# Token-major products in groups of 512 columns, and the relative-position vector copied from DRAM to DRAM

## The chip, the cores and the metric

The kernel runs on one core of a Trainium2 chip as one program. Its metric is the device time of one execution in microseconds (us): 1580.26 us, the median of three runs from 1579.17 to 1581.57.

Six kinds of instruction stream appear in the profile. PE is TensorE with its matmuls, PEld its weight loads (a matmul's stationary operand, 128 rows by 128 columns), DVE is VectorE, ACT is ScalarE, POOL is GpSimd, and SP is the queue that issues most transfers. Each stream runs its own instructions in order and waits for others by semaphores. 16 DMA engines carry the transfers of all streams.

## The reference

Two networks of two layers each run one after the other on 256 tokens of width 1024. The first has a gated recurrence beside a sliding-window attention, a cross attention to 256 memory tokens, and a gated feed-forward part. The second is what follows, cut to its core:

```python
def diff_attention(q, k, v, lam, rel_bias):
    ...
    bucket = t5_bucket(k_pos[None, :] - q_pos[:, None])
    bias = rel_bias[bucket].transpose(2, 0, 1)          # 4 heads, a value per distance
    p = softmax(einsum(q_blk, kt) + bias)
    w = p[:, :, 0] - lam * p[:, :, 1]
    return w @ v

for l in range(2):                                       # second_block
    h = rms_norm(x, pre_norm[l])
    proj = h @ w_in[l]
    y_a = rms_norm(diff_attention(q, k, v, lam, rel_bias)) * silu(z_a)
    y_h = hyena(u_h, x1, x2, filters) * silu(z_h)        # two FFT convolutions
    m = sigmoid(g_a) * (y_a @ w_pa[l]) + sigmoid(g_h) * (y_h @ w_ph[l])
    x = x + rms_norm(m @ w_out[l], post_norm[l])
```

Nearly all of the arithmetic is products of the 256 tokens with float32 weight matrices that are read from DRAM once, some 230 MB in all. The bias of an attention depends only on the distance between key and query, so it is a vector of 512 values for each of 4 heads.

## The kernel before

**Products in three parts.** A float32 product is made of three fp32r matmuls. Each operand is split into a rounded high part and the low rest. `mm3` adds high by high, high by low and low by high into the same PSUM tile.

**The weight stream.** `run_stream` takes the program as one list of chunks of weights, 1 MB each. SP loads a chunk into one of three raw buffers (L211). A chunk has two halves. For each half, ACT writes the high part (`wh`, L229) and DVE the low part (`wl`, L231), 128 partitions by 1024 values, into one of four pairs of split buffers. Then PE consumes the half. So a transfer that is late reaches PE by way of ACT.

**Two forms of product.** `fm` makes channel-major results: the weights are the stationary operand and the 256 tokens move, so every matmul has 256 columns. `tm` makes token-major results (256 tokens in two tiles of 128, `tb`): the activations are stationary and the weights move. It goes over the weight matrix in groups of 256 columns. A chunk is one group with all eight blocks of 128 rows (`k`), and its two halves are four blocks each. In a group each `tb` gets one PSUM tile of 256 columns, filled by 24 matmuls, and then the function `evac` empties it.

**Where `tm` stands.** In each layer of the first network: the queries with keys and values (`evq`, 1280 columns), the cross attention's values (`cross_v`), the mixer's output and the cross attention's output (both `out_proj`, with the layer norm in `ln_evac`). In each layer of the second: values and gate (`evv`, 1024 columns) and the output product (`evo`). In the last group of a `tm`, tile `tb` 0 is finished first, so that its `evac` can run while PE works on tile 1 (`hold`).

**Order.** PE and SP run in the order in which the program is written out. Attention, convolutions and norms are coroutines that `pump` lets go on between the halves of chunks, by a clock `self.t` that adds up the matmuls' columns. The other engines' order is set by a scheduler from priorities. PSUM has two pools of four banks: `pst` for `fm`, and `pch` for `tm` tiles and coroutines.

**The bias.** `load_bias` runs as part of `prep_co` beside the feed-forward part of the first network's second layer. A one-hot matmul gives the tile `vec` in PSUM, 4 heads by 512 values, which DVE copies to SBUF. One transfer from POOL's queue (L1200) then writes each head's row 128 times to a DRAM scratch tensor, `scr`, with the heads outermost: 4 x 128 x 512 values, 1 MB. Two further transfers (L1206) read it back with a row step of 511 instead of 512, so that partition p gets the row shifted by p. They fill the `bias` slots that `diff_co` adds to the scores in both layers of the second network.

Of the kernel before, what the change touches and what calls it, by code (L numbers as in the profile page):

```python
# [13 lines left out]
F32 = mybir.dt.float32  # L14
# [89 lines left out]
class Net:  # L104
# [300 lines left out]

    def tm(self, w, c0, ncols, x, evac):

        for c in range(c0, c0 + ncols, 256):
            box = {}
            last = c + 256 == c0 + ncols  # L410
            ci = (c - c0) // 256

            def part(h, tb, wt, ps):
                xx = x()
                t = slice(tb * P, tb * P + P)
                if self.start:

                    for j in range(3):
                        for k in range(4):
                            self.mm(ps, self.ch2(xx, k, t)[j == 1], wt[j == 2][:, k, :],  # L420
                                    k == 0 and j == 0, False)
                    self.start = tb == 0
                    return
                for k in range(4):
                    g = h * 4 + k
                    self.mm3(ps, self.ch2(xx, g, t), (wt[0][:, k, :], wt[1][:, k, :]),
                             g == 0, g == KD - 1)

            def first(wh, wl, box=box, last=last, part=part):
                box["ps"] = [self.pch([256], "tm") for _ in range(TB)]  # L430
                box["w"] = wh, wl
                part(0, 0, (wh, wl), box["ps"][0])
                if not last:
                    self.pump()
                    part(0, 1, (wh, wl), box["ps"][1])

            def second(wh, wl, box=box, last=last, part=part, ci=ci):
                part(1, 0, (wh, wl), box["ps"][0])
                evac(ci, 0, box["ps"][0])
                self.pump()  # L440
                if last:
                    part(0, 1, box["w"], box["ps"][1])
                part(1, 1, (wh, wl), box["ps"][1])
                evac(ci, 1, box["ps"][1])
            yield Chunk([(None, w[:, c:c + 256].rearrange("(k p) f -> p k f", p=P))], KD, 256,
                        False, [first, second], hold=last)

    def rstd(self, out, ss, scale, eps):
        if scale == 1.0:
# [83 lines left out]
        nc.vector.tensor_scalar(nsp, ab, -8.0, None, op0=ALU.mult)  # L533
        return sp, nsp

    def ln_evac(self, t, h, n=256, f=1.0, gb=None, pause=False):


        nc = self.nc
        st = {}  # L540

        def ev(c, tb, ps):
            if c == 0 and tb == 0:
                for b in range(TB):
# [282 lines left out]
    def mixer(self, l, s):  # L827
# [5 lines left out]
        def evq(c, tb, ps):  # L833
            if c == 0 and tb == 0:
                s.q = [self.slot("q", [D]) for _ in range(TB)]
                kvt = self.slot("kv", [2, TB, 256])
                s.kv, s.kT = kvt[:, 0], kvt[:, 1]
            dst = s.kv[:, tb, :] if c == 4 else s.q[tb][:, c * 256:c * 256 + 256]
            nc.scalar.activation(dst, ps, AF.Copy)
        yield from self.tm(w, 2048, 1280, x, evq)  # L840

# [54 lines left out]
    def cross_v(self, l, s):  # L896
        def ev(c, tb, ps):
            if c == 0 and tb == 0:
                s.V = [self.hl("cv", [D]) for _ in range(TB)]
            sl = slice(c * 256, c * 256 + 256)  # L900
            self.split(s.V[tb][0][:, sl], s.V[tb][1][:, sl], ps)
        return self.tm(self.a["ckv_w"][l], 1024, 1024, lambda: self.memT, ev)

# [59 lines left out]
    def ffn(self, l, s):  # L963
# [19 lines left out]
        def up(j):  # L983
            for i, c in enumerate((j * 256, D_FF + j * 256)):
                def ev(_, ps, i=i):
                    pss[j, i] = ps
                    if i == 1:
                        act(j)
                yield from self.fm(wi, c, 256, lambda: s.fx, ev)

        ev_ln = self.ln_evac(lambda: s.t, lambda: s.h, 512,
                             gb=lambda: s.gb, pause=l == DEPTH - 1)

        def down(j):
# [193 lines left out]
    def load_bias(self):  # L1188
# [7 lines left out]
        self.mm(ps, rb, oh, True, True)  # L1196
        vec = self.tmp([512], "vec")[:4, :]
        nc.vector.tensor_copy(vec, ps)
        flat = self.dr.tile([4, (P + 1) * 512], F32, name="scr")
        nc.gpsimd.dma_start(flat[:, :P * 512].rearrange("h (p r) -> h p r", r=512),  # L1200
                            vec[:, None, :].to_broadcast([4, P, 512]))
        self.bias = []
        for hp in range(2):
            b = self.slot("bias", [2, 384])
# [385 lines left out]
    def layer2(self, l, s, out):  # L1590
# [22 lines left out]
        def evv(c, tb, ps):  # L1613
            if c == 0 and tb == 0:
                s.v, s.za = self.slot("v", [TB, 512]), self.slot("za", [TB, 512])
            sl = slice((c % 2) * 256, (c % 2) * 256 + 256)
            if c < 2:
                nc.scalar.activation(s.v[:, tb, sl], ps, AF.Copy)
            else:
                z = s.za[:, tb, sl]  # L1620
                nc.scalar.activation(z, ps, AF.Tanh, scale=0.5)
                nc.vector.scalar_tensor_tensor(z, z, 1.0, ps, op0=ALU.add, op1=ALU.mult)
        yield from self.tm(w, 1024, 1024, x, evv)
# [27 lines left out]
        def begin():  # L1651
            if l < DEPTH - 1:
                self.load_pre_gain(l + 1)
            s.pn = self.slot("pn", [D])
            nc.gpsimd.dma_start(s.pn, a["post_norm_2"][l:l + 1, :].to_broadcast([P, D]))
            s.ss = [self.sm.tile([P, 4], F32, tag="pss", name=self.nm("pss")) for _ in range(TB)]
            s.xo = [self.slot("xo", [D]) for _ in range(TB)]
        yield begin

        def evo(c, tb, ps):  # L1660
            sl = slice(c * 256, c * 256 + 256)
            xo = s.xo[tb]
            jk = self.tmp([256], "jk2")
            nc.scalar.activation(jk, ps, AF.Square, accum_out=s.ss[tb][:, c:c + 1])
            nc.vector.tensor_tensor(xo[:, sl], ps, s.pn[:, sl], op=ALU.mult)
            if c == 3:
                sm = self.tiny(1, "sm")
                nc.vector.reduce_sum(sm, s.ss[tb], axis=AX)
                self.rstd(sm, sm, 1.0 / D, 4e-6)
# [99 lines left out]
```

## Time and profile before

| what | value |
|---|---|
| median of three runs | 1580.26 us (1579.17 to 1581.57) |
| the profiled execution's own time | 1578.38 us |
| its span, first to last instruction | 1576.6 us |
| PE, PEld busy | 96%, 92% of the span |
| DVE, ACT, POOL busy | 70%, 55%, 5% |
| mean granted clock of TensorE, share of full speed | 0.988 |
| matmuls and transposes | 11740 |

The shares say which engine is occupied over the whole span; where it is not, and why, is read from the waits and from windows of time. The page also cuts the span into 40 slices of 39.4 us and gives a tenth of busy time for each. A matmul's duration in the rows covers its pipeline from end to end, so that two that follow one another overlap; what one costs is read from the distance between the starts.

### The profile page before, as it was taken

To read this page: it belongs to the slowest core of one execution; us is meant where nothing else is said; L and a number is where in the kernel's file an instruction comes from. 1 tells how busy PE (TensorE), PEld (TensorE's weight loads), DVE (VectorE), ACT (ScalarE), POOL (GpSimd) and SP (SyncE) were. 2 spreads that over 40 slices of the span, in tenths; PEclk is the share of its full clock that TensorE was granted. 3 is DMA by queue.
4 is the path that set the end of the run, shared out by engine and by line. 5 is a ranking of instruction groups with operands and counts; after the bars stand their busy time and mean duration, and the time that the engine had idled before them with its cause. 6 is when DMAs were issued, how large, how long until landed. Compare 5 with 4: busy or idle time off the path is not lost. (4 is left out here: it accounts for less than half of the span.)

```text
span 1576.6 us, 28159 instructions
## 1 busy us (share of the span) xinstructions
PE 1513.9 (96%) x11740; PEld 1446.1 (92%) x11740; DVE 1103.9 (70%) x1642; ACT 867.7 (55%) x1378; POOL 83.5 (5%) x151
## 2 busy tenths in 40 slices
PE   8999999999999999999999999948999999999997
PEld 7889999999999999899999989947799899898997
DVE  5867677667655578767777875514897978797865
ACT  5789444535444446794446466513545665555753
POOL 4001000000000000010000200000000010000000
PEclk9999999999999999999999999978999999999999
DMA  9434755545555554356564775536355346354452
GB/s 278 135 122 147 234 179 177 165 157 201 175 186 188 187 161 155 108 180 214 187 187 161 208 217 184 183 69 206 110 165 171 120 154 208 128 166 140 142 167 80
DMA packets 228304, 264.09 MB, mean 168 GB/s; under 512 B 6231, under 2 KB 213305, under 8 KB 228176
## 3 DMA queue, kind: packets, MB, share of 16 engines
q1 hardware_dynamic: 221808, 246.43, 48.6%
q0 software_dynamic: 6368, 15.85, 4.2%
q8 instruction: 92, 1.51, 0.4%
q14 instruction: 36, 0.29, 0.1%
HBM read 260.16 MB, written 2.10 MB: 166 GB/s over the span
## 5 line engine op out<-in xcount | busy, mean ns | idle before, releaser
L231 DVE TENSOR_TENSOR wl<-raw,wh 128x1024 fp32r<-128x1024 f32 x464 | 568.1, 1227 | 326.0 <-ACT wh L229 321.2
L229 ACT ACTIVATE wh<-raw 128x1024 fp32r<-128x1024 f32 (+1 forms) x465 | 490.4, 1058 | 468.5 <-PE fm L361 241.9
L361 PE MATMUL fm<-h2h,wh 128*128 128x256 f32 x704 | 172.6, 286 | 27.5 <-ACT wh L229 27.5
L361 PE MATMUL fm<-n2h,wh 128*128 128x256 f32 x640 | 176.6, 286 | 1.2 <-ACT n2h L350 1.2
L361 PE MATMUL fm<-n2l,wh 128*128 128x256 f32 x640 | 174.8, 283 | 1.4 <-DVE n2l L351 1.4
L361 PE MATMUL fm<-n2h,wl 128*128 128x256 f32 x640 | 174.5, 283 | 0.0
L361 PE MATMUL fm<-h2h,wl 128*128 128x256 f32 x704 | 171.7, 285 | 0.5 <-DVE wl L231 0.5
L361 PE MATMUL fm<-h2l,wh 128*128 128x256 f32 x704 | 171.6, 285 | 0.4 <-DVE h2l L351 0.4
L361 PEld LDWEIGHTS fm<-h2h,wh 128*128 128x128 f32 x704 | 124.5, 194 | 32.0 <-ACT wh L229 27.9
L361 PEld LDWEIGHTS fm<-h2h,wl 128*128 128x128 f32 x704 | 123.5, 194 | 0.8 <-DVE wl L231 0.8
L361 PEld LDWEIGHTS fm<-h2l,wh 128*128 128x128 f32 x704 | 123.5, 194 | 0.6 <-DVE h2l L351 0.6
L361 PEld LDWEIGHTS fm<-n2h,wh 128*128 128x128 f32 x640 | 119.9, 192 | 3.3 <-ACT n2h L350 1.7
L361 PEld LDWEIGHTS fm<-n2l,wh 128*128 128x128 f32 x640 | 119.8, 192 | 1.8 <-DVE n2l L351 1.8
L361 PEld LDWEIGHTS fm<-n2h,wl 128*128 128x128 f32 x640 | 119.9, 192 | 0.2
L361 PE MATMUL tm<-wh,mgl 128*128 128x256 f32 x256 | 72.5, 283 | 0.7 <-DVE mgl L351 0.7
L361 PE MATMUL tm<-wl,mgh 128*128 128x256 f32 x256 | 72.4, 283 | 0.0
L361 PE MATMUL tm<-wh,mgh 128*128 128x256 f32 x256 | 72.4, 283 | 0.0
L361 PE MATMUL fm<-xTh,wh 128*128 128x256 f32 x256 | 70.9, 287 | 0.0
L361 PE MATMUL fm<-h3h,wh 128*128 128x256 f32 x256 | 70.8, 287 | 0.0
L361 PE MATMUL fm<-h3h,wl 128*128 128x256 f32 x256 | 69.8, 283 | 0.0
L361 PE MATMUL fm<-xTh,wl 128*128 128x256 f32 x256 | 69.8, 283 | 0.0
L361 PE MATMUL fm<-h3l,wh 128*128 128x256 f32 x256 | 69.8, 283 | 0.0
(432 smaller groups left out, 4073.3 us busy)
## 6 DMA issues: line engine op xcount, KB each, us to landing
raw<-in_w_in_dram SPq DMA_DIRECT2D x89, 1024.0 KB, 5.3
raw<-in_ffn_wi_dram SPq DMA_DIRECT2D x44, 1024.0 KB, 5.2
raw<-in_ffn_wo_dram SPq DMA_DIRECT2D x22, 1024.0 KB, 5.0
raw<-in_w_out_dram SPq DMA_DIRECT2D x16, 1024.0 KB, 5.3
raw<-in_ckv_w_dram SPq DMA_DIRECT2D x16, 1024.0 KB, 5.3
raw<-in_w_br_attn_dram SPq DMA_DIRECT2D x8, 1024.0 KB, 5.4
raw<-in_w_br_rnn_dram SPq DMA_DIRECT2D x8, 1024.0 KB, 5.3
raw<-in_cq_w_dram SPq DMA_DIRECT2D x8, 1024.0 KB, 5.2
```

The source lines that it names most:

```text
L229: hi_ins = self.nc.scalar.activation(hi[:, i:i + q], s[:, i:i + q], AF.Copy)
L231: lo_ins = self.nc.vector.tensor_tensor(lo, s, hi.bitcast(F32), op=ALU.subtract)
L361: self.nc.tensor.matmul(out, lhsT=l, rhs=r, start=start, stop=stop)
```

## The change

Two places change. In `load_bias`, `vec` is first written to a small DRAM tensor, `row`, of 4 x 512 values (8 KB). The transfer into `scr` then reads `row` instead of the SBUF tile and has the 128 copies outermost, the heads second.

In `tm` a group has 512 columns where 512 are left (the 1280 columns of `evq` become 512, 512 and 256). A chunk of a 512-column group has four blocks of 128 rows, so that it is 1 MB as before, and a group takes two chunks. Each half has two blocks. The functions that empty PSUM handle 512 columns at a time, and the norms' partial sums get half as many parts.

```diff
-        for c in range(c0, c0 + ncols, 256):
+        end = c0 + ncols
+        for gi, c in enumerate(range(c0, end, 512)):
+            wd = min(512, end - c)
+            nk = 2048 // wd
             box = {}
-            last = c + 256 == c0 + ncols
-            ci = (c - c0) // 256
...
-                for k in range(4):
-                    g = h * 4 + k
-                    self.mm3(ps, self.ch2(xx, g, t), (wt[0][:, k, :], wt[1][:, k, :]),
-                             g == 0, g == KD - 1)
+                for i in range(n):
+                    k = g * n + i
+                    self.mm3(ps, self.ch2(xx, k, t), (wt[0][:, i, :], wt[1][:, i, :]),
+                             k == 0, k == KD - 1)
...
+            def half(g, hold, wh, wl, box=box, part=part, gi=gi, wd=wd, nk=nk):
+                n_half = 2 * KD // nk
+                if g == 0:
+                    box["ps"] = [self.pch([wd], "tm") for _ in range(TB)]
+                part(g, 0, (wh, wl))
+                if hold and g == n_half - 2:
+                    box["w"] = wh, wl
+                    return
+                if g == n_half - 1:
+                    evac(gi, 0, box["ps"][0])
                 self.pump()
-                if last:
-                    part(0, 1, box["w"], box["ps"][1])
-                part(1, 1, (wh, wl), box["ps"][1])
-                evac(ci, 1, box["ps"][1])
+                if hold and g == n_half - 1:
+                    part(g - 1, 1, box["w"])
+                part(g, 1, (wh, wl))
+                if g == n_half - 1:
+                    evac(gi, 1, box["ps"][1])
+            for ck in range(KD // nk):
+                hold = c + wd == end and ck == KD // nk - 1
+                src = w[ck * nk * P:(ck + 1) * nk * P, c:c + wd]
...
-    def ln_evac(self, t, h, n=256, f=1.0, gb=None, pause=False):
+    def ln_evac(self, t, h, n=512, f=1.0, gb=None, pause=False):
...
+        one = self.dr.tile([4, 512], F32, name="row")
+        nc.gpsimd.dma_start(one, vec)
         flat = self.dr.tile([4, (P + 1) * 512], F32, name="scr")
-        nc.gpsimd.dma_start(flat[:, :P * 512].rearrange("h (p r) -> h p r", r=512),
-                            vec[:, None, :].to_broadcast([4, P, 512]))
+        nc.gpsimd.dma_start(flat[:, :P * 512].rearrange("h (p r) -> p h r", r=512),
+                            one[None, :, :].to_broadcast([P, 4, 512]))
...
-            sl = slice(c * 256, c * 256 + 256)
+            sl = slice(c * 512, c * 512 + 512)
             xo = s.xo[tb]
-            jk = self.tmp([256], "jk2")
+            jk = self.tmp([512], "jk2")
```

What this does to the order of the engines is shown at three places. The first is POOL's stream around the bias, before the change (`scr` and `bias` as above, `up` the borders of the second network's convolution inputs):

```order
L1191 DMA oh_11401<-in_c_bucket_dram 32x512
L1200 DMA scr<-vec_11491 4x128x512
L1501 MEMSET up_12258 128x2
...
L1502 MEMSET up_12611 128x2
L1206 DMA bias_11495<-scr 128x2x384
L1206 DMA bias_11497<-scr 128x2x384
```

And the same place after it:

```order
L1200 DMA oh_10545<-in_c_bucket_dram 32x512
L1210 DMA row<-vec_10635 4x512
L1212 DMA scr<-row 128x4x512
L1218 DMA bias_10641<-scr 128x2x384
L1218 DMA bias_10643<-scr 128x2x384
L1513 MEMSET up_11404 128x2
```

There is one transfer more, the large one has 128 as its first size instead of 4, and the two that read the copies back stand right behind it, ahead of the borders.

The second place is PE's stream at the start of the first layer's output product (`tm` the PSUM tile of a token tile, `wh` and `wl` the weights' parts, `mgh` and `mgl` the activations'), before the change:

```order
L361 MATMUL tm_2678<-wh_2571,mgh_2469 128x256
L361 MATMUL tm_2678<-wl_2572,mgh_2469 128x256
L361 MATMUL tm_2678<-wh_2571,mgl_2471 128x256
...
L361 MATMUL tm_2679<-wh_2571,mgh_2469 128x256
L361 MATMUL tm_2679<-wl_2572,mgh_2469 128x256
...
L361 MATMUL tm_2678<-wh_2603,mgh_2470 128x256
```

And after it:

```order
L361 MATMUL tm_2574<-wh_2467,mgh_2365 128x512
L361 MATMUL tm_2574<-wl_2468,mgh_2365 128x512
L361 MATMUL tm_2574<-wh_2467,mgl_2367 128x512
...
L361 MATMUL tm_2575<-wh_2467,mgh_2365 128x512
L361 MATMUL tm_2575<-wl_2468,mgh_2365 128x512
...
L361 MATMUL tm_2574<-wh_2499,mgh_2365 128x512
```

A tile now gets six matmuls of 512 columns from a half where it got twelve of 256. Over the program 2400 `tm` matmuls of 256 columns become 1152 of 512 and 96 of 256; nothing else on PE changes its order.

The third place is DVE's stream at the end of the same product (`t` the sum with the residual, `bst` the statistics, `mv` and `rs` mean and scale), before the change:

```order
L548 SCALAR_TENSOR_TENSOR t_2676<-x_99,tm_2808 128x256
L550 BN_STATS bst_2720<-t_2676 128x6
L548 SCALAR_TENSOR_TENSOR t_2677<-x_100,tm_2809 128x256
L550 BN_STATS bst_2721<-t_2677 128x6
L231 TENSOR_TENSOR wl_2867<-raw_2670,wh_2866 128x1024
L548 SCALAR_TENSOR_TENSOR t_2676<-x_99,tm_2872 128x256
L550 BN_STATS bst_2720<-t_2676 128x6
L553 BN_AGGR mv_2900<-bst_2720 128x2
```

And after it:

```order
L231 TENSOR_TENSOR wl_2645<-raw_2503,wh_2644 128x1024
L231 TENSOR_TENSOR wl_2665<-raw_2566,wh_2664 128x1024
L231 TENSOR_TENSOR wl_2681<-raw_2566,wh_2680 128x1024
L557 SCALAR_TENSOR_TENSOR t_2572<-x_99,tm_2650 128x512
L559 BN_STATS bst_2632<-t_2572 128x6
L562 BN_AGGR mv_2700<-bst_2632 128x2
```

The last sum and statistics before the mean now cover 512 columns each, and the sums of the third quarter no longer stand ahead of them.

## Rows read from the trace of the kernel before

**Rows 1.** The page: engine busy time, share and instruction count.
```profile
PE 1513.9 (96%) x11740; PEld 1446.1 (92%) x11740; DVE 1103.9 (70%) x1642; ACT 867.7 (55%) x1378; POOL 83.5 (5%) x151
```

**Rows 2.** The page's 40 slices: granted clock and DMA share, in tenths.
```profile
PEclk9999999999999999999999999978999999999999
DMA  9434755545555554356564775536355346354452
```

**Rows 3.** PE's waits: line, releaser, us in total, times, longest.
```profile
PE fm L361 <- ACT wh L229: 27.5, 1, 27.5
...
PE dft L361 <- DVE dsc L1420: 3.5, 2, 1.8
PE tx L373 <- DVE xn L1579: 2.3, 1, 2.3
PE tx L373 <- DVE t L562: 2.1, 3, 1.4
```

**Rows 4.** Timeline of ACT: start us, us, instruction, idle before and releaser.
```profile
1070.43 2.01 ACT L229 ACTIVATE wh<-raw 128x1024 fp32r<-128x1024 f32 x2 [36.04 <-DMA raw<-in_ffn_wi_dram]
```

**Rows 5.** DMA issues: queue, count, KB each, median us to landing.
```profile
raw<-in_ffn_wi_dram SPq DMA_DIRECT2D x44, 1024.0 KB, 5.2
...
fdl<-in_flt_deltas_dram POOLq DMA_DIRECT2D x4, 512.0 KB, 8.2
...
scr<-vec POOLq DMA_DIRECT2D x1, 1024.0 KB, 47.5
...
bias<-scr POOLq DMA_DIRECT2D x2, 384.0 KB, 5.8
...
fb<-in_flt_bias_dram POOLq DMA_DIRECT2D x4, 2.0 KB, 2.8
```

**Rows 6.** Timeline of SP and POOL: issues around the wait.
```profile
1022.41 1.13 POOL L1200 DMA_DIRECT2D scr<-vec  x1 [83.76 <-DVE vec L1198]
...
1023.27 6.60 SPq L211 DMA_DIRECT2D raw<-in_ffn_wi_dram  x2
```

**Rows 7.** Windows: from:to us, busy us (instructions) PE, PEld, DVE, ACT, POOL, clock, DMA, GB/s.
```profile
1044.00:1065.00 21.00, 0.04 (x1) 0.00 (x0) 0.00 (x0) 0.00 (x0) 0.00 (x0) 0.59 0.27 32
...
1071.00:1078.00 7.00, 6.00 (x26) 5.70 (x27) 5.83 (x6) 3.96 (x5) 0.13 (x2) 0.50 0.47 165
```

**Rows 8.** Timeline of PE after the wait, first row and first at full pace.
```profile
1071.54 0.80 PE L361 MATMUL fm<-h2h,wh 128*128 128x256 f32 x2 [27.50 <-ACT wh L229]
...
1078.51 0.29 PE L361 MATMUL fm<-h2h,wl 128*128 128x256 f32 x1
```

**Rows 9.** Chain that ended last: start us, us, engine, tile, instructions.
```profile
1193.25 10.08 PE tm L361 x84
...
1544.51 20.18 PE tm L361 x168
```

**Rows 10.** Timeline of PE in the feed-forward part's 512-column matmuls.
```profile
1104.81 0.39 PE L361 MATMUL ff<-wh,al 128*128 128x512 f32 x1
...
1110.02 0.39 PE L361 MATMUL ff<-wl,ah 128*128 128x512 f32 x1
```

**Rows 11.** Groups by shape: count, busy us, mean ns, idle before.
```profile
L550 DVE BATCH_NORM_STATS2 bst<-t 128x6 f32<-128x256 f32 x32 | 13.6, 426 | 1.0
...
L548 DVE SCALAR_TENSOR_TENSOR t<-t,tm 128x256 f32<-128x256 f32 x24 | 9.8, 410 | 1.7 <-PE tm L361 1.7
...
L548 DVE SCALAR_TENSOR_TENSOR t<-t,ff 128x512 f32<-128x512 f32 x8 | 5.2, 673 | 0.0
...
L550 DVE BATCH_NORM_STATS2 bst<-t 128x6 f32<-128x512 f32 x8 | 5.1, 679 | 0.0
```

**Rows 12.** The same view of ACT.
```profile
L350 ACT ACTIVATE cqh<-fm 128x512 fp32r<-128x512 f32 x8 | 4.8, 598 | 14.5 <-PE fm L361 14.5
...
L1664 ACT ACTIVATE jk<-tm 128x256 f32<-128x256 f32 x16 | 6.2, 385 | 17.0 <-PE tm L361 17.0
```

More of the change, by code (lines that the diff above doesn't have):

```diff
@@ L406, in tm, with part @@
     def tm(self, w, c0, ncols, x, evac):
-        for c in range(c0, c0 + ncols, 256):
+        end = c0 + ncols
+        for gi, c in enumerate(range(c0, end, 512)):
+            wd = min(512, end - c)
+            nk = 2048 // wd
             box = {}
-            last = c + 256 == c0 + ncols
-            ci = (c - c0) // 256
-            def part(h, tb, wt, ps):
+            def part(g, tb, wt, box=box, nk=nk):
                 xx = x()
+                ps = box["ps"][tb]
                 t = slice(tb * P, tb * P + P)
+                n = nk // 2
                 if self.start:
                     for j in range(3):
-                        for k in range(4):
+                        for k in range(n):
                             self.mm(ps, self.ch2(xx, k, t)[j == 1], wt[j == 2][:, k, :],
@@ L423, in part @@
                     return
-                for k in range(4):
-                    g = h * 4 + k
-                    self.mm3(ps, self.ch2(xx, g, t), (wt[0][:, k, :], wt[1][:, k, :]),
-                             g == 0, g == KD - 1)
[L429 to L435, printed above, removed]
@@ L437, in second @@
-            def second(wh, wl, box=box, last=last, part=part, ci=ci):
-                part(1, 0, (wh, wl), box["ps"][0])
-                evac(ci, 0, box["ps"][0])
-                self.pump()
-                if last:
-                    part(0, 1, box["w"], box["ps"][1])
-                part(1, 1, (wh, wl), box["ps"][1])
-                evac(ci, 1, box["ps"][1])
-            yield Chunk([(None, w[:, c:c + 256].rearrange("(k p) f -> p k f", p=P))], KD, 256,
-                        False, [first, second], hold=last)
+                for i in range(n):
+                    k = g * n + i
+                    self.mm3(ps, self.ch2(xx, k, t), (wt[0][:, i, :], wt[1][:, i, :]),
+                             k == 0, k == KD - 1)
@@ L448, in rstd @@
+            for ck in range(KD // nk):
+                hold = c + wd == end and ck == KD // nk - 1
+                src = w[ck * nk * P:(ck + 1) * nk * P, c:c + wd]
+                yield Chunk([(None, src.rearrange("(k p) f -> p k f", p=P))], nk, wd, False,
+                            [lambda wh, wl, f=half, g=2 * ck + h, o=hold: f(g, o, wh, wl)
+                             for h in range(2)], hold=hold)
     def rstd(self, out, ss, scale, eps):
@@ L837, in evq @@
                 s.kv, s.kT = kvt[:, 0], kvt[:, 1]
-            dst = s.kv[:, tb, :] if c == 4 else s.q[tb][:, c * 256:c * 256 + 256]
+            dst = s.kv[:, tb, :] if c == 2 else s.q[tb][:, c * 512:c * 512 + 512]
             nc.scalar.activation(dst, ps, AF.Copy)
@@ L989, in up @@
                 yield from self.fm(wi, c, 256, lambda: s.fx, ev)
-        ev_ln = self.ln_evac(lambda: s.t, lambda: s.h, 512,
+        ev_ln = self.ln_evac(lambda: s.t, lambda: s.h,
                              gb=lambda: s.gb, pause=l == DEPTH - 1)
@@ L1615, in evv @@
                 s.v, s.za = self.slot("v", [TB, 512]), self.slot("za", [TB, 512])
-            sl = slice((c % 2) * 256, (c % 2) * 256 + 256)
-            if c < 2:
-                nc.scalar.activation(s.v[:, tb, sl], ps, AF.Copy)
+            if c == 0:
+                nc.scalar.activation(s.v[:, tb, :], ps, AF.Copy)
             else:
-                z = s.za[:, tb, sl]
+                z = s.za[:, tb, :]
                 nc.scalar.activation(z, ps, AF.Tanh, scale=0.5)
@@ L1655, in begin @@
             nc.gpsimd.dma_start(s.pn, a["post_norm_2"][l:l + 1, :].to_broadcast([P, D]))
-            s.ss = [self.sm.tile([P, 4], F32, tag="pss", name=self.nm("pss")) for _ in range(TB)]
+            s.ss = [self.sm.tile([P, 2], F32, tag="pss", name=self.nm("pss")) for _ in range(TB)]
             s.xo = [self.slot("xo", [D]) for _ in range(TB)]
@@ L1660, in evo @@
         def evo(c, tb, ps):
-            sl = slice(c * 256, c * 256 + 256)
+            sl = slice(c * 512, c * 512 + 512)
             xo = s.xo[tb]
-            jk = self.tmp([256], "jk2")
+            jk = self.tmp([512], "jk2")
             nc.scalar.activation(jk, ps, AF.Square, accum_out=s.ss[tb][:, c:c + 1])
             nc.vector.tensor_tensor(xo[:, sl], ps, s.pn[:, sl], op=ALU.mult)
-            if c == 3:
+            if c == 1:
                 sm = self.tiny(1, "sm")
```

## The prediction

> **What bounds the kernel now.** I read the engines' shares first, then the slices, then PE's waits, and then followed the longest of these back. PE is busy for 1513.9 of 1576.6 us [rows 1]. So a matmul saved is time saved, unless a supplier of PE becomes late, and 62.7 us are left in which PE does nothing. The reader is to see in the slices that the granted clock stands at nine tenths or more except in two, the 28th and 29th, from about 1064 us, and that the DMA share falls to 3 and 4 tenths just before [rows 2]. PE's waits name one long one, 27.5 us, for a `wh` of ACT [rows 3]. ACT itself had waited 36.04 us, for a raw chunk of the feed-forward weights [rows 4].
>
> Why that chunk was late: SP issued it at 1023.27 us [rows 6], ACT took it up at 1070.43 [rows 4], so it was 47.2 us on its way, where the median of its kind is 5.2 [rows 5]. POOL had issued the transfer into `scr` at 1022.41, and that took 47.5 us to land [rows 5, 6]. Both end at about the same moment. While PE stood still the DMA share was 0.27 [rows 7], about 4 of 16 engines, and `scr` is written with 4 heads outermost. I read this as: the copies occupy four engines, a weight chunk is spread over all sixteen, and its four parts on those engines land only when the copies are through.
>
> **The wait that goes.** PE stopped at 1071.54 - 27.50 = 1044.04. It did not come back at full pace: the clock was 0.50 in the window 1071 to 1078, that is 1.2 GHz, after 27.5 us without work, and rows at the short distance begin at 1078.51 [rows 7, 8]. Between the two rows stand 28 matmuls of 256 columns (twelve rows of two and four single ones). At full pace a 256-column matmul costs 10.08 / 84 = 120.0 ns by the chain [rows 9], so the 28 need 3.4 us. If the wait goes, the instruction of 1078.51 starts at 1044.04 + 3.4 = 1047.4: **31.1 us** less, of which 27.5 is the wait and 3.6 the slow return.
>
> Whether it goes rests on the new transfer, of which there is no row. Its 1 MB spread over sixteen engines takes 47.5 x 4 / 16 = 11.9 us if each engine keeps its pace of now. Below, a weight chunk of the same size takes 5.2 us. Above, 512 KB of `fdl`, also one DRAM row read for 128 places, take 8.2 us, so 1 MB would take 16.4 [rows 5]. I take 11.9, worked out from the transfer itself. Ahead of it comes the small transfer into `row`, some 2.8 us by the nearest of that size (`fb`), and POOL waits for it.
>
> What PE can bear: ACT started the late chunk 1.1 us ahead of PE's return [rows 4, 8], so it was needed by 1042.9, 19.6 us after its issue; 5.2 of these it needs, 14.4 are spare. The next chunk was issued at about 1029.5, the end of the pair's row less 0.4 us [rows 6], and is needed one chunk of PE (48 matmuls, 5.8 us) later, so at 1048.7. A transfer of T us that starts at about 1026 and goes wholly ahead of it lets it land at 1031 + T. PE waits only if T is over some 17 us; none of the three values is. What queues behind the new waits on POOL are the reads into `bias` and small borders that the second network wants 90 us later. The two reads of 384 KB (5.8 us each) now follow at once instead of at 1090, beside weights: they are part of the risk of a short wait, below. So I take the whole 31.1.
>
> By the Trainium skill, "DMA: Bandwidth & Descriptors", section "Why a DMA increments its semaphore by 16 and not by 1", the number of engines is the largest up to 16 that divides the slowest size on both sides. That is 4 before and 16 after; the 0.27 agrees, and no row can show the 16.
>
> **Wider groups.** Of `tm`'s 2400 matmuls of 256 columns 96 stay, and 2304 become 1152 of 512. The cost of one of 512 is seen in the feed-forward part, where the starts run from 1104.81 to 1110.02 over 23 steps: 226.5 ns [rows 10]. Two of 256 cost 240.0; the last stage's 168 in 20.18 us give the same 120.1 [rows 9]. So 13.5 ns go with each pair: 1152 x 13.5 = **15.6 us**. Products, bytes, split instructions and their sizes stay. A half of a chunk costs PE 2.72 us instead of 2.88, and ACT and DVE must split one in that time. Fewer and longer evacuations make their work slightly less.
>
> A rule that speaks against this: the Trainium skill, "TensorE: Matmul & The Clock Gate", section "Back-to-back issue gap", gives 262 cycles for 256 columns and 518 for 512. That is 2.5 ns for a pair, an estimate of 2.9 us in all. The rows do not agree: they have 13 ns beyond the columns' own time on either size, each matmul here having its own weight load, and the measurement decides.
>
> **Longer ends.** A product ends with the emptying of its last group, which now has 512 columns on DVE's path instead of 256, and the earlier columns are no longer done before.
>
> - Layer norms. The sum rises from 410 to 673 ns and the statistics from 426 to 679 [rows 11], 0.52 us for a token tile. The two tiles follow one another on DVE, and PE arrives 0.16 us earlier for want of twelve matmuls' gain. PE already waited for this end three times, 2.1 us in all [rows 3], so there is no slack: about 1.05 us for each of four norms, 4.2 us.
> - The output products of the second network. ACT's square goes from 385 to about 598 ns (another 512-column read of PSUM) [rows 12], and DVE's product by about 0.26 as the sums do: 0.5 us, paid between the layers, where PE waits 2.3 us already [rows 3], and at the very end. With the 0.16: 1.1 us.
> - The gate. Its last column group is emptied just before the attention's first scores, for which PE waits 1.8 us in each layer now [rows 3]; 0.5 us longer each, 1.0 us.
>
> Together **6.3 us** given back. Bounds: nothing, if DVE's high-priority work fits into gaps; 12, if each end moves the work behind it too.
>
> **Sum.** 1578.4 (the profiled execution) - 31.1 - 15.6 + 6.3 = 1538.0. That execution is 1.9 us below the median, so for the median: **1540 us**. Own range, by the 12 and the nothing of the ends and 2 us for placement: 1532 to 1547.
>
> **Rivals.**
>
> - *A short wait stays.* The copies, now on all engines, with the two reads behind them, delay the weights for longer than the spare 14 us. For: the pace of DRAM to DRAM has no row, and what was a queue on four engines becomes one on sixteen. Against: 11.9 us by the pace, and weights issued before the copies go first. A wait of 6 us with its slow return of some 3: about 1549. The Trainium skill says in the same DMA page, section "Issuing engines are not separate DMA queues", that transfers from all queues interleave on the same sixteen engines; that would make this shorter.
> - *The wider groups give nothing*, because PE in `tm` turns out to be paced by weight splits or PSUM banks held twice as long. For: a bank now stays taken for some 11 us instead of 6, and coroutines use the same four. Against: 120.0 ns holds throughout the stages. 1540 + 15.6 = 1556. By the estimate from the Trainium skill's page it would be 1553.
> - *The copies are not spread* and go on occupying four engines. The wait stays and starts 2.8 us later: 1540 + 31.1 + 2.8 = 1574.
> - *The copies are slow in DRAM itself*, and hold all sixteen engines. Each microsecond of T beyond 47.5 less the 2.8 then adds to the wait of now. Since the groups give 15.6 - 6.3 = 9.3 us net, the kernel is slower from T = 47.5 - 2.8 + 9.3 = 54 us on, a pace a quarter of what I took. If reading and writing each take the 47.5 us, T is 95 and the time 1580.3 + 41 = 1621. Against: the transfer of now moves the same bytes into the same tensor and leaves twelve engines free for weights at their usual pace.
>
> **How the numbers follow.** Forecast 0.73, short wait 0.09, groups without gain 0.09, not spread 0.05, slow in DRAM 0.04. A change of under 0.2% (3.2 us) can't be told from none. The first three are all faster; of the not-spread case I give 0.03 to faster and 0.02 to the same, since it sits 6 us from the median: faster 0.94, same 0.02, slower 0.04. The range 1532 to 1556 leaves out the last two cases (0.09) and some of the ends' uncertainty, some 0.18 in all.
>
> **What would show it.** `scr<-row` landing in about 12 us with a DMA share near 1; no PE wait above 3 us in the feed-forward part and a clock that stays at 1.00 there; starts of `tm` matmuls 226 to 227 ns apart; PE's waits on `t`, `xn` and `dsc` 5 to 7 us above today's. A wait of 10 us or more for a raw chunk, or a `tm` distance above 235 ns, would prove me wrong.

## The result, and the profile after

The changed kernel takes 1541.07 us (median of 4 runs, 1539.51 to 1541.46) against 1579.72 us before (4 runs beside them, 1578.79 to 1581.57): a ratio of 0.9752, 95% interval 0.9735 to 0.9769. Forecast were 1540 us, faster. The profiled execution took 1541.07 us with a span of 1539.3 us, 37.3 us less than the span before. The total came out; two of the reasons behind it did not, as the experiments show.

The page of the changed kernel, engine shares and the two lines of slices that answer to [rows 1, 2]:

```profile
PE 1504.5 (98%) x10588; PEld 1386.0 (90%) x10588; DVE 1094.9 (71%) x1590; ACT 862.4 (56%) x1338; POOL 83.6 (5%) x152
...
PEclk9999999999999999999999999999999999999999
DMA  8435655545555555446565475575355356354442
```

1152 matmuls are gone, and the slices of reduced clock with them. PE's waits (line, releaser, us in total, times, longest) no longer hold the one of 27.5 us of [rows 3], nor that of the second convolution's transform (`dft`) on `dsc`; those on `t` and `xn` have grown:

```profile
PE tx L373 <- DVE t L571: 5.1, 3, 2.4
...
PE tx L373 <- DVE xn L1591: 3.0, 1, 3.0
...
PE tm L361 <- ACT wh L229: 1.3, 1, 1.3
...
PE ds L361 <- DVE dsc L1432: 0.9, 2, 0.5
```

The transfers around the copies (queue, count, KB, median us to landing), against [rows 5]:

```profile
scr<-row POOLq DMA_DIRECT2D x1, 1024.0 KB, 6.9
...
bias<-scr POOLq DMA_DIRECT2D x2, 384.0 KB, 3.8
...
row<-vec POOLq DMA_DIRECT2D x1, 8.0 KB, 2.1
```

While they ran, from 1023 to 1030 us, the DMA share was 0.93 and the clock 1.00:

```profile
1023.00:1030.00 7.00, 7.00 (x53) 6.67 (x52) 3.41 (x3) 2.53 (x3) 0.54 (x1) 1.00 0.93 337
```

The chain shows the new distance of `tm` (start, us, engine, tile, instructions): 10.89 / 48 = 226.9 ns and 19.08 / 84 = 227.1, where [rows 9] give 120.0 for half the columns, so 13.1 ns for each of 1152 pairs, 15.1 us:

```profile
1172.14 10.89 PE tm L361 x48
1284.64 19.08 PE tm L361 x84
```

And the evacuations, as groups by shape, against [rows 11, 12]:

```profile
L559 DVE BATCH_NORM_STATS2 bst<-t 128x6 f32<-128x512 f32 x24 | 15.7, 684 | 0.2
L557 DVE SCALAR_TENSOR_TENSOR t<-t,tm 128x512 f32<-128x512 f32 x12 | 7.9, 681 | 1.2 <-PE tm L361 1.2
L1675 ACT ACTIVATE jk<-tm 128x512 f32<-128x512 f32 x8 | 4.8, 599 | 12.4 <-PE tm L361 12.4
```

**Where the time went.** The 9340 matmuls outside `tm` are the same in both kernels, one for one. How far each starts earlier than before, place by place, gives the account: +31.3 us at the bias wait, +15.1 from the `tm` distance (taken out of each place by its count of pairs), and -9.1 at the ends, which is what the span leaves (31.3 + 15.1 - 37.3). The ends, in us: the four norms -1.1, -0.4, +0.1 and -2.5 (-3.9); between the second network's layers -2.3 and at the very end -0.8; the start -1.4, the cross attention's values -0.6 and output -0.8; one stretch near 926 us -1.5; the gate and the stage behind it +2.0 (more on all three below). Each figure is rounded.

### The profile page after: what moved, and what is told of

It is laid out like the page before. It is cut to its first block, busy times and chain, and to the rows that moved or that the text cites. A ratio compares the mean times of both kernels' runs of the same rounds, so it can differ in the third digit from the quotient of the medians.

```text
span 1539.3 us, 25749 instructions
## 1 busy us (share of the span) xinstructions
PE 1504.5 (98%) x10588; PEld 1386.0 (90%) x10588; DVE 1094.9 (71%) x1590; ACT 862.4 (56%) x1338; POOL 83.6 (5%) x152
## 5 line engine op out<-in xcount | busy, mean ns | idle before, releaser
L361 PE MATMUL fm<-xTl,wh 128*128 128x256 f32 x256 | 69.8, 283 | 0.0
L361 PE MATMUL ff<-wh,ah 128*128 128x512 f32 x176 | 69.1, 392 | 0.0
L361 PE MATMUL ff<-wl,ah 128*128 128x512 f32 x176 | 68.7, 390 | 0.0
```

Source lines behind the costliest of these rows:

```text
L361: self.nc.tensor.matmul(out, lhsT=l, rhs=r, start=start, stop=stop)
```

## The experiments

**1. The copies alone** (the kernel before with the new transfer, all groups of 256 columns).

```
+one = self.dr.tile([4, 512], F32, name="row")
+nc.gpsimd.dma_start(one, vec)
-nc.gpsimd.dma_start(flat...("h (p r) -> h p r"), vec[:, None, :].to_broadcast([4, P, 512]))
+nc.gpsimd.dma_start(flat...("h (p r) -> p h r"), one[None, :, :].to_broadcast([P, 4, 512]))
```

> The kernel before with only the copies of the relative-position vector changed (one row in DRAM, then DRAM to DRAM, rows outermost); every product keeps its groups of 256 columns. My theory: the wait of 27.5 us and the slow return after it go whole, and nothing else moves, so about 31 us less than before: 1548.5 us, no wait of PE above 3 us in the feed-forward part, and the copies land in about 7 us, as they did in the changed kernel. Rival: part of the 31 us gained at this place in the changed kernel came from the wider groups (fewer, longer emptyings beside it). Then this kernel gains clearly less, 25 us or under: 1555 us or more.

Measured: 1550.40 us (1549.46 to 1550.82), ratio 0.9820 [0.9804, 0.9836]; copies in 7.0 us, and PE waits for no weights in the feed-forward part. At the place itself the matmuls start 31.3 us earlier, as in the changed kernel, so the rival falls. But the span shrank by 28.2 only. Of the other 3 us 2.7 went in two stretches near 647 and 930 us (1.3 and 1.5), where nothing was changed. Windows of the kernel before (from:to us, busy us and instructions of PE, PEld, DVE, ACT and POOL, granted clock, DMA share, GB/s) at both places:

```profile
646.00:650.00 4.00, 3.82 (x26) 2.71 (x27) 0.75 (x3) 4.00 (x13) 0.00 (x0) 1.00 0.63 219
...
928.00:932.00 4.00, 3.96 (x25) 3.24 (x26) 3.22 (x4) 3.76 (x5) 0.89 (x2) 1.00 0.02 4
```

and of this kernel:

```profile
647.00:651.00 4.00, 3.95 (x21) 3.63 (x20) 1.52 (x3) 3.90 (x12) 0.00 (x0) 0.57 0.47 166
...
929.50:933.50 4.00, 3.95 (x15) 3.04 (x15) 2.51 (x3) 2.82 (x4) 0.00 (x0) 0.60 0.02 4
```

The clock column is the point: 1.00 in one execution, 0.57 and 0.60 in another of the same instructions (a stretch of 3.4 us at 1.2 GHz lies inside each window). These two stretches are there in one execution and not in the other. They follow pauses of PE (some 2 us at the first place, 1.3 us at the second), which both executions have.

**2. The groups alone** (the changed kernel with the old transfer: the edit of experiment 1 undone).

> The changed kernel with the old transfer of the copies, so that only the groups of 512 columns are left of the change. My theory: 15.1 us less by the closer starts and 9.1 us given back at the ends, as the two traces add up, so 6 us less than before: 1574 us, with the long wait of PE of some 28 us and its slow return still there. Rival: the two parts help each other (the chunks are asked for earlier, or the ends cost less beside the long wait), and the sum of the two parts alone differs from the whole change by more than 3 us: then this kernel is at 1577 us or above, or at 1571 us or below.

Measured: 1572.17 us (1570.74 to 1574.56), ratio 0.9960 [0.9944, 0.9976], PE's wait 27.2 us; the span is 5.9 us below that of before. As forecast: the groups alone bring 6 us, and the long wait does not depend on them:

```profile
PE fm L361 <- ACT wh L229: 27.2, 1, 27.2
```

The two parts alone make 28.2 + 5.9 = 34.1 us against 37.3 together. The missing 3.2 us are within what the slow stretches of experiment 1 make up: the two profiles of the parts have four of them near these two places, the changed kernel's has one, and each costs some 1.3 to 1.5 us. An effect of the two parts on each other below that size is not excluded.

**3. Heads outermost, source in DRAM.**

```
-nc.gpsimd.dma_start(flat...("h (p r) -> p h r"), one[None, :, :].to_broadcast([P, 4, 512]))
+nc.gpsimd.dma_start(flat...("h (p r) -> h p r"), one[:, None, :].to_broadcast([4, P, 512]))
```

> The changed kernel, with its row in DRAM, but with the 4 heads outermost in the transfer of the copies, so that the source is the new one and the order the old one. Theory A, the order alone decides, each engine keeps the pace of the transfer before (47.5 us on 4 engines): the copies land in about 47 us, the DMA share beside PE's wait is near 0.27, the wait is about 28 us, and the time is about 1572 us. Theory B, order and source both decide: at the 6.9 us that the changed kernel's transfer took on sixteen engines, four engines need about 28 us; the wait of PE is 3 to 11 us with a slow return of up to 3, and the time is 1545 to 1555 us. Rival, the source alone decides: it lands in some 7 us, no wait above 3 us, and 1541 us.

Measured: 1539.66 us (one run). Copies in 15.1 us; no wait of PE for weights in the feed-forward part. The issue's row:

```profile
scr<-row POOLq DMA_DIRECT2D x1, 1024.0 KB, 15.1
```

and from ACT's timeline (start us, us, instruction, idle before and releaser) the one split that had to wait for its chunk, by 1.5 us, while PE still had work:

```profile
1039.27 1.06 ACT L229 ACTIVATE wh<-raw 128x1024 fp32r<-128x1024 f32 x1 [1.50 <-DMA raw<-in_ffn_wi_dram]
```

Theory A, which was the prediction's, is refuted: with the order of before the wait is gone. Besides the source, and the groups, which leave the wait as it was (experiment 2), only the small transfer ahead differs, which lets the copies start later; experiment 7 bears on that. The order does matter to the landing (15.1 against 6.9 us) but not to the time.

**4. Rows outermost, source in SBUF.**

```
-nc.gpsimd.dma_start(flat...("h (p r) -> p h r"), one[None, :, :].to_broadcast([P, 4, 512]))
+to = flat...("h (q k r) -> q k h r", q=16)
+six = [self.slot("six", [2, 512])[:16] for _ in range(2)]   # each filled from row, for 16 partitions
+for h in range(4):
+    nc.gpsimd.dma_start(to[:, :, h, :], six[h // 2][:, None, h % 2, :].to_broadcast([16, 8, 512]))
```

> The changed kernel, with rows outermost as there, but out of SBUF: the row is first read into 16 partitions (2 x 64 KB), and each head's 128 copies are written from these, 8 from each partition, in four transfers of 256 KB. The prediction reckoned with 16 engines at the pace of the transfer before (SBUF to DRAM, 47.5 us on 4 engines): 11.9 us for the 1 MB. If that pace belongs to the source in SBUF, the last of the four transfers lands 10 to 14 us after the first is issued. If the pace was that of a few partitions read over and over or of the order, and the source does not matter on 16 engines, about 7 us as in the changed kernel. If SBUF as a source holds the whole transfer to one pace whatever the engines, 30 us or more, and a PE wait of over 10 us. In the first two cases the time is that of the changed kernel, 1541 us.

Measured: 1542.04 us (one run). On POOL's timeline the four transfers are issued from 1028.26 on, and the read that needs the last two follows at 1041.66: 13.4 us, the first of the three cases.

```profile
1028.26 2.13 POOL L1217 DMA_DIRECT2D scr<-six  x4 [3.92 <-DMA six<-row]
1036.46 0.76 POOL L1223 DMA_DIRECT2D bias<-scr  x1 [6.07 <-DMA scr<-six]
1041.66 0.72 POOL L1223 DMA_DIRECT2D bias<-scr  x1 [4.45 <-DMA scr<-six]
```

So the 11.9 us of the prediction was about right for SBUF as the source; the pace goes with the source. From 1034 to 1040 us 144 packets of 4 KB kept sixteen engines busy for 95.7%, some 0.64 us each; from 1032 to 1034, at the start, 109 of them took 0.28 us each on average, and why is open. Whether it is the memory that sets the pace, or each engine's reading of one partition over and over, was not separated. The same 1 MB lands in 47.5 us (SBUF, 4 engines), 13.4 (SBUF, 16), 15.1 (DRAM, 4) and 6.9 (DRAM, 16). Either half of the change, with the small transfer ahead of it, removes PE's wait.

**5. and 6. Holding four engines longer.** First the copies of experiment 3 made twice, in two transfers:

```
+two = self.dr.tile([4, (P + 1) * 512], F32, name="two")
-nc.gpsimd.dma_start(flat...)
+for to in (two, flat):
+    nc.gpsimd.dma_start(to...("h (p r) -> h p r"), one[:, None, :].to_broadcast([4, P, 512]))
```

> The changed kernel with the 4 heads outermost and the source in DRAM, as in the run before with 15.1 us, but the copies are made twice, into two tensors, one after the other (the first is read by nothing). My theory: a weight chunk issued behind the copies lands when the four engines have done with them (in the run with one copy the chunk of 1027.1 landed after 12.1 us, with the copies), so with two the chunk lands at about 1051 instead of 1039; ACT splits it 12 us late, PE waits 10 to 11 us and returns at 1.2 GHz for some 2 to 3: about 1553 us. Rival: queues share an engine evenly, or the long wait of before belonged to the source in SBUF alone; then the chunk lands in 12 us or less again, and there is no wait above 3 us: 1540 us.

Measured: 1542.42 us (one run), no wait. The two transfers landed in 15.2 and 18.6 us, side by side: POOL's queue took 43.0% of 16 engines from 1030 to 1036 us, more than four engines can give. They ran on different engines, so the question was not put. The Trainium skill has a rule that fits ("DMA: Bandwidth & Descriptors", section "Why a DMA increments its semaphore by 16 and not by 1"): a transfer issued by POOL that is spread over fewer than 16 engines takes its engines from a cursor that moves on. Then one transfer of twice the size:

```
-flat = self.dr.tile([4, (P + 1) * 512], F32, name="scr")
+flat = self.dr.tile([4, (2 * P + 1) * 512], F32, name="scr")
+nc.gpsimd.dma_start(flat[:, :2 * P * 512]...("h (p r) -> h p r"), one[:, None, :].to_broadcast([4, 2 * P, 512]))
```

> The changed kernel with the 4 heads outermost and the source in DRAM, and 256 copies of each head in one transfer of 2 MB instead of 128 in 1 MB (the second half is read by nothing). In the run with two transfers of 1 MB the second found other engines: the DMA share was about 0.5 and both were through 19 us after the first one's issue, so it did not put the question. One transfer should keep to its four engines. My theory: the copies land about 28 us after their issue at 1022.7 (15.1 for the first half, some 13 for the second), the DMA share falls to about 0.25 once the weights on the other engines are through, the chunk issued at 1027 lands only then, at about 1050, and PE waits for it for about 10 us and comes back at 1.2 GHz for some 2 to 3 us more: about 1552 us. Rival: a transfer whose source lies in DRAM lets the weights past, whatever its length, and the long wait of before belonged to the source in SBUF: then the chunk lands in 12 to 14 us or less, no wait above 3 us, 1540 us.

Measured: 1542.44 us (one run), again no wait of PE. My theory failed: the copies held their engines for 29.8 us, yet the chunk issued at 1028.5 was there at 1046.5, when they still had 7 us to go. ACT waited for it, PE did not:

```profile
1046.53 2.01 ACT L229 ACTIVATE wh<-raw 128x1024 fp32r<-128x1024 f32 x2 [7.38 <-DMA raw<-in_ffn_wi_dram]
```

What happens instead stands in the DMA queues' packets. The kernel before, from 1046 to 1058 us, in the middle of PE's wait (q0 is POOL's queue with the copies, q1 SP's with the weights; packets, MB, share of 16 engines):

```profile
DMA packets 144, 0.37 MB, mean 31 GB/s; under 512 B 0, under 2 KB 72, under 8 KB 144
...
q0 software_dynamic: 72, 0.29, 23.5%
q1 hardware_dynamic: 72, 0.07, 1.7%
```

72 packets of each: the queues take turns on an engine, one packet each, though one is of 4 KB and the other of 1 KB. From the shares, a packet of the copies takes 0.235 x 16 x 12 us / 72 = 627 ns and one of the weights 45. A chunk of 1 MB in 1 KB packets has 64 on each of 16 engines, so on the four engines that also copy it needs 64 turns of 0.67 us, 43 us, as long as the copies last.

In the kernel before they did not last that long. The weights' queue there from 1024 to 1034 us, and from 1069 to 1071:

```profile
q1 hardware_dynamic: 1553, 1.57, 48.1%
...
q1 hardware_dynamic: 164, 0.16, 23.5%
```

The 1.57 MB are three quarters of the two chunks issued at 1023.3 and 1029.5, what the other twelve engines carry of them. So on the four engines the first chunk's turns began only at about 1034, some 11 us after its issue; why is open. At a turn in 0.67 us, over 50 of its 64 packets an engine went in turns with the copies, and the rest at once when these were through at 1069.9, as the second row shows (164 packets in 2 us, where there had been 12). That is why both ended together: the end of the copies did release the last packets, but most of the chunk had not waited for it.

In the long transfer out of DRAM a turn is short. While the chunk of 1028.5 was on its way, from 1039.5 to 1040.5 us:

```profile
q0 software_dynamic: 21, 0.09, 20.9%
...
q1 hardware_dynamic: 21, 0.02, 6.0%
```

A packet of the copies took 0.209 x 16 / 21 = 159 ns and one of the weights 46, so 64 turns are an estimated 13 us of the 18 that this chunk took.

The Trainium skill states the turns ("DMA: Bandwidth & Descriptors", section "Queues, rings and completion order"): each engine goes round its queues packet by packet. The trace agrees; where the page counts some 9 to 17 descriptors to a turn, the profile's records alternate one for one.

**7. The old transfer doubled** (the kernel before, source in SBUF, 256 copies of each head).

```
-flat = self.dr.tile([4, (P + 1) * 512], F32, name="scr")
+flat = self.dr.tile([4, (2 * P + 1) * 512], F32, name="scr")
+nc.gpsimd.dma_start(flat[:, :2 * P * 512]..., vec[:, None, :].to_broadcast([4, 2 * P, 512]))
```

> The kernel before with 256 copies of each head in its one transfer (2 MB, out of SBUF, heads outermost) instead of 128; the second half is read by nothing. My prediction's reading was that a weight chunk's parts on the four engines land only when the copies are through. The packets of the runs so far say otherwise: from 1046 to 1058 us of the kernel before, the four engines carried 72 packets of the copies (4 KB, 627 ns each) and 72 of the weights (1 KB, 46 ns), turn and turn about. A chunk has 64 packets on each engine, so it lands after 64 turns of 0.67 us = 43 us, whatever the copies still have to do; in the kernel before these have 64 packets an engine too, so both ended together. If turns decide, the first chunk lands after some 47 us as before and PE waits 27 to 28 us; the next chunk needs 64 more turns, and PE waits a second time, 43 us less the 6 to 9 us that it works on one chunk: 33 to 37 us. If the copies go first, there is one wait of about 70 us and no second. Either way the time is near 1578 + 43 = 1621 us, and copies land in about 91 us.

Measured: 1612.35 us (one run); copies in 93.1 us, through at 1119. Two waits of PE (their sum, their number, the longest), but not those I gave:

```profile
PE fm L361 <- ACT wh L229: 48.6, 2, 41.4
```

The first ends with this split of ACT's timeline:

```profile
1093.90 2.00 ACT L229 ACTIVATE wh<-raw 128x1024 fp32r<-128x1024 f32 x2 [49.87 <-DMA raw<-in_ffn_wi_dram]
```

The chunk issued just behind the copies escaped this time, and the next one, of 1033.3, was late: it landed at 1093.9, 25 us before the copies were through. That rules out "copies first". It also shows that a first chunk that gets through ahead of the copies is not enough to spare PE: with the source in SBUF PE stood still for the chunk behind. The late chunk's packets alternate with the copies' for as long as it lasts (1060 to 1088 us):

```profile
q0 software_dynamic: 168, 0.69, 23.5%
q1 hardware_dynamic: 168, 0.17, 1.7%
```

64 turns are 43 us, from 1050 to 1093; why these did not begin until some 16 us after the issue stays open, as the 11 us of the kernel before do.

**8. The low parts held back behind the norm.** In the changed kernel DVE's timeline at the second layer's norm reads

```profile
880.28 0.69 DVE L559 BATCH_NORM_STATS2 bst<-t 128x6 f32<-128x512 f32 x1
880.90 0.67 DVE L351 TENSOR_TENSOR h2l<-tx,h2h 128x512 fp32r<-128x512 f32 x1
881.49 0.20 DVE L562 BATCH_NORM_AGGREGATE mv<-bst 128x2 f32<-128x12 f32 x1
881.60 0.63 DVE L351 TENSOR_TENSOR h2l<-tx,h2h 128x512 fp32r<-128x512 f32 x1
882.16 0.14 DVE L459 TENSOR_SCALAR rs<-mv 128x1 f32<-128x1 f32 x1
```

with two subtractions inside the norm's chain, for whose end PE waits 2.44 us by its timeline:

```profile
884.34 1.78 PE L373 MATMUL tx<-ident,t 128*128 128x128 f32 x8 [2.44 <-DVE t L571]
```

The edit:

```
-yield from self.to_fm_block(t, hT, 0)
+yield from self.to_fm_block(t, hT, 0, self.normed if (l, i) == (1, 2) else None)
 # split(): the subtraction is issued after that instruction
```

> The changed kernel, with the four subtractions that make the low parts of the first token tile, ahead of the feed-forward part of the second layer, held back on DVE until the norm of both tiles is done. In the changed kernel two of them (0.67 and 0.63 us) stand between the statistics of the second tile and its normalising, and PE waits 2.4 us for that tile, where before it waited 0.4; a stretch of 1.2 GHz of 3.4 us follows. My theory: of this end's 4.0 us some 2 to 3 come from that order and the slow stretch behind it; so PE waits about 1.2 us, the slow stretch goes, and the kernel needs 2 to 3 us less than the changed one: 1538.5 us. Rival: the wait comes from the wider statistics and sums alone, and the subtractions only move: then the wait stays above 2 us, and the time is within 1 us of the changed kernel or above it, since the feed-forward part gets its low parts later.

Measured: 1540.26 us (1539.12 to 1541.20), ratio 0.9756 [0.9742, 0.9771]: no gain to be told. The order changed as meant, and PE's wait fell from 2.44 to 1.55 us:

```profile
885.16 1.32 PE L374 MATMUL tx<-ident,t 128*128 128x128 f32 x8 [1.55 <-DVE t L572]
```

but the stretch at 1.2 GHz behind it stayed (clock 0.57 from 886 to 890 us), and the low parts came later. The 0.9 us were given back on the spot.

**9. Narrow last groups.**

```
-for gi, c in enumerate(range(c0, end, 512)):
-    wd = min(512, end - c)
+cols = list(range(c0, end, 512)) + ([end - 256] if narrow else [])
+for gi, c in enumerate(cols):
+    wd = min(512, (cols + [end])[gi + 1] - c)
 # narrow=True for four output projections and two output products
```

> The changed kernel, but the last 512 columns of the output projections ahead of a norm and of the second network's output product are done as two groups of 256 again (six products, whose last half is read by ACT and DVE in the old sizes); all else keeps 512. It gives up 6 x 48 pairs x 13.1 ns = 3.8 us of PE. My theory: the ends cost what they cost because of the wide last group, so the waits on t and xn go back to those of before (2.1 and 2.3 us) and some 8 us come back, most of it at the second layer's norm (4.0) and between the networks' layers (3.1): 4 us less than the changed kernel, 1537 us. Rival: a part of what the ends gave back is no end at all but stretches of 1.2 GHz that come and go from one execution to the next (the kernel with the copies alone had two, of 3.4 us, in code that is the same as before and ran without them). Then the waits get shorter by 3 us in all and the rest stays: 1541 to 1542 us, no gain.

Measured: 1535.53 us (5 runs, 1534.99 to 1536.56), ratio 0.9719 [0.9705, 0.9732], the fastest of all. The interval lies below the changed kernel's, by little. The waits went back to those of [rows 3]:

```profile
PE tx L373 <- DVE xn L1596: 2.3, 1, 2.3
PE tx L373 <- DVE t L576: 2.2, 3, 1.5
```

Place by place, the norms came back by 1.1, 0.4, 1.1 and 2.5 us and the step between the layers by 1.9; 288 pairs at 13.1 ns, 3.8 us, were paid. Windows of the changed kernel at the second layer's norm, near 926 us and between the second network's layers:

```profile
884.00:888.00 4.00, 3.66 (x18) 3.31 (x19) 2.85 (x5) 1.19 (x2) 3.40 (x6) 0.59 0.83 249
924.00:929.00 5.00, 4.78 (x19) 3.39 (x19) 3.54 (x5) 4.09 (x6) 0.27 (x1) 0.66 0.05 10
1310.00:1318.00 8.00, 5.82 (x18) 4.96 (x19) 6.61 (x13) 4.84 (x11) 1.10 (x2) 0.58 0.00 0
```

and of this one:

```profile
884.00:888.00 4.00, 3.60 (x28) 3.16 (x27) 3.61 (x6) 1.75 (x4) 2.08 (x4) 1.00 0.90 259
924.00:929.00 5.00, 5.00 (x34) 4.03 (x33) 4.20 (x5) 3.52 (x4) 1.19 (x2) 1.00 0.31 111
1310.00:1318.00 8.00, 7.41 (x41) 6.25 (x40) 6.17 (x8) 5.22 (x10) 0.55 (x1) 0.86 0.15 39
```

The slow stretch at the norm is gone, and the one between the layers is half as long. Of the stretches elsewhere, the one near 926 us is gone (1.5 us), but one near 643 us has come (1.4), so they nearly cancel in this pair of profiles. The mean granted clock of every run says the same of the whole: 0.995 to 0.999 in the five runs of this kernel, 0.991 to 0.995 in the four of the changed one.

## Why the prediction was right, and where it was wrong

- **The wait that goes: 31.1 us forecast, 31.3 measured.** The size was right, wait and slow return both, since these were read off PE's own rows. The cause was half right: four engines were indeed the place (0.27), but the step "its four parts on those engines land only when the copies are through" failed as a rule. The parts take turns with the copies, packet for packet, and a turn was long because a 4 KB packet out of SBUF took 627 ns; out of DRAM it took 159. In the kernel before, only the last packets of the chunk waited for the copies' end, and in experiment 7 a chunk landed 25 us ahead of it.
- **"PE waits only if T is over some 17 us"** was wrong with it: 29.8 us on four engines made no wait (experiment 6). There the first chunk was also issued 1.8 us ahead of the copies, thanks to the small transfer into `row`, whereas [rows 6] have it 0.9 us behind them. The head start alone is not the reason: in experiment 7 the first chunk escaped too, and PE waited 41.4 us for the next. How much it adds to the short turns was not separated.
- **T = 11.9 us; measured 6.9.** "If each engine keeps its pace of now" was the step that failed. The pace went with the source, which I had treated as the same. From SBUF, sixteen engines took 13.4 (experiment 4), close to the term. It cost nothing, as all of these lie below what PE can bear. On sixteen engines the wait goes with the source in SBUF as well (experiment 4), so that it went is not luck.
- **The groups: 15.6 forecast, 15.1 measured** (13.1 ns a pair for 13.5). The rival that they give nothing falls (experiment 2). The Trainium skill's 2.5 ns a pair ("TensorE: Matmul & The Clock Gate", section "Back-to-back issue gap"), an estimate of 2.9 us in all, isn't what these runs show.
- **The ends: 6.3 forecast, 9.1 measured, and made up differently.** Norms 3.9 for 4.2, but uneven, 2.5 of it in one place where the order on DVE changed and a stretch at 1.2 GHz followed. The output products 3.1 for 1.1: after PE's 3.0 us on `xn` the clock stood at 0.58 from 1310 to 1318 us, where the wait of 2.3 us in [rows 3] was followed by 1.00. The first products and the cross attention, 2.8, which I had not listed at all. The stretch near 926, 1.5, is no end. All seven profiles with wide last groups have it, but so have those of experiments 1 and 7, whose groups are of 256 columns; the kernel before and experiment 9 lack it. So whether it is the change's is open. And the gate with the wrong sign: I forecast a loss of 1.0, it gained 0.6 in each layer, and a further 0.9 lies behind the first. The step that failed is a reading: the row of `dsc` in [rows 3] is a wait of the transform's matmuls (`dft`), not of the scores, as I took it. That wait of 3.5 us vanished, and about 1.0 us came back before the next scores (`ds`); why was not tested. That these misses add up to only 2.8 us is luck: 4.3 that I had not listed and 2.0 at the output products stand against 3.0 at the gate. Experiment 9 confirms the width as a cause at the norms and between the layers, where half of the slow stretch stayed; at the norms more came back (5.1 us) than the wide groups had cost there (3.9).
- **The signs to look for**: a DMA share near 1 (0.93), no long wait in the feed-forward part, clock 1.00 there, starts 227 ns apart: all as written. The waits on `t`, `xn` and `dsc` were to grow by 5 to 7 us; `t` and `xn` grew by 3.7 and `dsc` fell by 2.6.
- **A misreading without effect**: the slices of reduced clock in [rows 2] are the 27th and 28th, from about 1025 us, and the DMA share is 3 tenths in the first of them and 6 in the second. No term of the sum rests on it.

The total came close because the two large terms were right and the misses at the ends partly cancel. Against the 1538.0 of the sum the profiled execution took 3.1 us more: 0.2 less at the wait, 0.5 more in the groups, 2.8 more at the ends.

## What to carry to other kernels

A transfer on few engines is dangerous less by its bytes than by the time of one of its packets: whoever shares an engine with it pays one such packet per packet of its own, so look at the source and the packet size, and not at the number of engines alone. When two things end together, don't conclude that one waited for the other; count what each moved meanwhile. Wide groups save PE a few nanoseconds an instruction everywhere, but the last group before a dependent stage is better narrow.

## What the runs showed of the hardware

- 1 MB of copies: 47.5, 13.4, 15.1 and 6.9 us by source (SBUF, SBUF, DRAM, DRAM) and engines (4, 16, 4, 16); the second in four transfers.
- Two queues on one engine alternated record by record, 72 to 72 and 168 to 168, though the records are of 4 KB and of 1 KB. Before that the later queue moved nothing on the shared engines for some 11 and 16 us (kernel before, experiment 7).
- Stretches of 3.4 or 6.8 us at 1.2 GHz appear after pauses of PE of some 1.3 to 3 us. All seven profiles of kernels with wide last groups have one at the second layer's norm, near 926 us and between the second network's layers; experiment 9's has one of 3.4 us between the layers too, and experiments 1 and 7 have one near 930 us. Near 645 us they come in one execution and not in the next, with the same instructions. Each of 3.4 us costs some 1.3 to 1.5 us, so differences under some 2 us between two single profiles prove nothing.
